# Output projection and first gate/up matrices of a hybrid encoder layer: side work as one list of timed events, four operands split in place, spatial matmuls interleaved

## The chip, the cores and the metric

The kernel is one program on one core of a Trainium2 chip. The time is the device time of one execution in microseconds (us). The engines of the core run their own instruction streams in order and wait for each other by semaphores: PE (TensorE, matmuls and transposes), DVE (VectorE), ACT (ScalarE), POOL (GpSimd) and SP (SyncE). Here SP issues nearly all DMA transfers, one after the other, and an issue that must wait holds back the issues behind it.

## The reference, cut to what matters

Two sequences of 1024 tokens (16 tiles of 128 tokens, 1024 wide) go through one encoder layer in fp32:

```python
h = rms_norm(x, norm1)
proj = h @ w_in                                   # q, k, v, gu, gv
a = rms_norm(windowed_gqa(q, k, v, ...), attn_out_gain)
g = rms_norm(chunked_spatial_gating(gu, gv, v_gain, w_s, b_s), gmlp_out_gain)
x = x + concatenate([a, g], -1) @ w_o             # output projection
h2 = rms_norm(x, norm2)
x = x + (silu(h2 @ w_gate) * (h2 @ w_up)) @ w_down
```

In `chunked_spatial_gating` each of 8 heads has a full 128x128 matrix that mixes the positions of a chunk: `s = einsum("hpq,bcqhd->bcphd", w_s, vh) + b_s`, and the result is `gelu(u) * s`.

## The kernel before

Every fp32 product is made of three fp16 (or fp32r) matmuls of split operands: a high part `hi`, which ACT casts, and a low part `lo = src - hi`, which DVE subtracts (`split16`, lines 112 to 114: one ACT and one DVE instruction each).

The stages that the change touches come after the attention:

**Gating loop**, `for t in range(NT)`. Tile `t` gets the products gv and gu (`gm_pieces`, 24 matmuls each). After every fourth tile, at t = 5, 9 and 13, `gm_group` applies the spatial matrices to a group of four tiles: 8 heads, 3 matmuls each into one of the 4 banks of the PSUM pool `psx`; DVE empties a bank with 2 instructions (line 684) before the fifth head can use it again. In between, `wo_step` and `wo_step2` load two rows of blocks of w_o (tiles `wr`, line 730), scale them on ACT (line 731) and split them.

**Output projection**, `for n in range(8): o_pair(n, ...)`. A pair is two tiles, q and q+4 of one sequence. The 2x2 block product is made of seven block products instead of eight, so a pair is 7 products of 12 matmuls, `o_product(ops, 0..6, ...)`. Its seven operands come from `o_turn`: load the two `mix` tiles (attention and gating halves, from DRAM), transpose them on PE (16 transposes `pm`), add and subtract blocks, and split. The finished rows `xr` are stored (`x1_d`), normalised (`o_norm`: square on ACT, power on POOL, scale on ACT into `xs`), and then `o_h2` transposes them (8 transposes `ph` for each tile), copies them to `hf` with the gain (8 small ACT instructions, line 957), forms the sums and differences of blocks and stores seven operands `B11, T2, B21, T3, T1, T4, B22` in DRAM (`t_d`).

**Gate/up matrices**, `matrix(n)`. The FFN's gate and up products have the same form: 7 products of 12 matmuls for each (weight pair, gate or up, sequence). Their operands `tops[s, i]` are read back from `t_d` (`top_load`: two loads of 512 KB for each operand into tiles `tr`) and split (`top_conv`: a cast on ACT and a subtraction on DVE of 1024 columns each). Operands 0 to 3 of a sequence lie in two tiles of the pool `big` (4 slots of 16 KB a partition), operands 4 to 6 in the pool tag L. The first two matrices (weight pair 0) run for sequence 0 alone, the next two (weight pair 1) for sequence 0 and then two for sequence 1. `prep_op` makes the seven weight operands of a matrix.

The order is the program order of the Python calls, refined by the framework's own scheduler: it keeps the emitted order as a priority and fills gaps. What stands between the products is set by hand: `POS = ['', 't', '', '0', '1', '']` says what follows each product of a pair: `o_turn` of the next pair after product 1, `o_h2` of the previous pair's two tiles after products 3 and 4. `pair_hooks` adds loads and conversions of sequence 0's operands for pairs 4 to 7; the rest of them, the preparation of the first weight operands and the last pair's `o_h2` come after pair 7. `top_step` does one load or conversion of sequence 1's operands after each product of the first four matrices.

The tags of the pool `k4p` limit what is in flight: XL has 3 slots (`mix` and `tr` share them), XN 3 (`xr`, and weights `raw` of up matrices), S 9, M 8, L 12.

Of the kernel before, what the change touches and what calls it, by code (L numbers as in the profile page):

```python
# [35 lines left out]
POS = ['', 't', '', '0', '1', '']  # L36
# [15 lines left out]

TW = {
# [11 lines left out]
def kernel(  # L65
# [461 lines left out]
    def gm_pieces(t, z):  # L527
        nm_ = ("gv", "gu")[z]
        if z == 0:
            pxg[t] = k4("S", f"xg{t}", (P, 2, GW))  # L530
        elif t % GROUP:
            pxg[t] = grp[t // GROUP][0][t % GROUP // 2][:, t % 2, :]
        ps = mm(f"p{nm_}{t}", [P, GW])
        for k in range(KD):
            mm3(ps, hT[t](k), wgl[nm_][0][:, k, :], wgl[nm_][1][:, k, :], k == 0, k == KD - 1)
            yield
        if z:
            dst = pxg[t] if t % GROUP else pxg[t][:, 1]
# [244 lines left out]
    def o_turn(n):  # L783
        xts, pms = [], []
        for t in pairs[n]:
            mx_ = k4("XL", f"mix{t}")
            load(mx_[:, 0:AW], mix_a[t])
            load(mx_[:, AW:D], mix_g[t])
            for z in range(2):
                pt = xx(f"pm{t}_{z}", [P, 4, P])  # L790
                for j in range(4):
                    k = z * 4 + j
                    nc.tensor.transpose(pt[:, j, :], mx_[:, k * P : (k + 1) * P], ident)
                pms.append(pt)
        for t in pairs[n]:
            xt = k4("XN", f"xr{t}")
            load(xt, xn[t])
            xts.append(xt)
        sc = h16(f"sc{n}", (P, 8, 4, P), F32)
        a11, a12, p21, a22 = pms  # L800
        a21, s1, s2, s3, s4 = (sc[:, i] for i in range(5))
        tl = [k4("S", f"mo{n}_{i}", (P, 2, 2, 4, P), F16) for i in range(4)]
        ops = [(tl[i // 2][:, i % 2, 0], tl[i // 2][:, i % 2, 1]) for i in range(7)]
        split16(*ops[0], a11)
        split16(*ops[2], a12)
        nc.scalar.copy(a21, p21)
        nc.vector.tensor_add(s1, a22, a21)
        split16(*ops[5], a22)
        nc.vector.tensor_sub(s3, a11, a21)
        nc.vector.tensor_sub(s2, s1, a11)  # L810
        split16(*ops[1], s2)
        nc.vector.tensor_sub(s4, a12, s2)
        split16(*ops[3], s3)
        split16(*ops[4], s1)
        split16(*ops[6], s4)
        st_b[n] = (xts, sc, ops)

    for t in range(NT):
        if t + 1 < NT and t + 1 >= NFILL:
            split_x(t + 1)  # L820
        if t >= NFILL:
            run(gm_pieces(t, 0))
        if t % GROUP:
            if t == 1:
                gm_chain(0)
            if t % GROUP != 1 or t == 1:
                gm_chain(t)
        if t > GROUP and t % GROUP == 1:
            gm_group(t // GROUP - 1)
            gm_chain(t - 1)  # L830
            gm_chain(t)
        if t == NT - 1:
            o_turn(0)
# [40 lines left out]
    def o_norm(t, xt):  # L874
        store(x1_d[t], xt)
        xs = k4("L", f"xs{t}")
        ms = small("a_ms", 1)
        nc.scalar.activation(xs, xt, AF.Square, scale=1.0 / 32.0, accum_out=ms)
        r2 = rsqrt_mean("a", ms, 1, EPS)
        nc.scalar.mul(xs, xt, r2)  # L880
        st_b["x", t] = xs

    def o_pair(n, hooks=()):
        (x_t, x_u), sc, ops = st_b.pop(n)
# [7 lines left out]
        def half(j):  # L892
            if n >= 1:
                o_h2(pairs[n - 1][j])

        def turn():
            if n + 1 < len(pairs):
                o_turn(n + 1)

        def extra(i):  # L900
            for fn in hooks[i] if hooks else ():
                fn()
            for c in POS[i]:
                if c == "0":
                    half(0)
                elif c == "1":
                    half(1)
                else:
                    turn()

        pa = mm(f"wa{n}", [P, 512])
        o_product(ops, 0, pa, True, True)
        nc.scalar.copy(u2, pa)
        extra(0)
        pb = mm(f"wb{n}", [P, 512])
        o_product(ops, 1, pb, True, True)
        nc.vector.tensor_add(u2, pb, u2)
        extra(1)
        o_product(ops, 2, pa, False, True)
        done(x_t, 0, pa)  # L920
        extra(2)
        pc = mm(f"wc{n}", [P, 512])
        o_product(ops, 3, pc, True, True)
        nc.scalar.copy(p7, pc)
        extra(3)
        pd = mm(f"wd_{n}", [P, 512])
        o_product(ops, 4, pd, True, True)
        nc.scalar.copy(p5, pd)
        nc.vector.tensor_add(p7, p7, u2)
        extra(4)  # L930
        o_product(ops, 5, pc, False, True)
# [4 lines left out]
        o_norm(pairs[n][1], x_u)  # L936
        extra(5)
        o_product(ops, 6, pd, False, True)
        nc.vector.tensor_add(u2, pd, u2)
        done(x_t, 1, u2)  # L940
        o_norm(pairs[n][0], x_t)

    hfs = {}

    def o_h2(t):
        s, i = divmod(t, TS)
        half, q = divmod(i, 4)
        xs = st_b.pop(("x", t))
        hf = k4("L", f"hf{t}", (P, KD, P))
        for z in range(2):  # L950
# [4 lines left out]
            for j in range(4):  # L955
                k = z * 4 + j
                nc.scalar.mul(hf[:, k, :], pt[:, j, :], n2s[:, k : k + 1])
        cs = slice(q * P, (q + 1) * P)
        if half == 0:
            hfs[t] = hf  # L960
            store(t_d[s][B11][:, :, cs], hf[:, 0:4, :])
            store(t_d[s][B21][:, :, cs], hf[:, 4:8, :])
# [3 lines left out]
        store(t_d[s][B22][:, :, cs], b22)  # L966
# [6 lines left out]
        for op, src in ((T1, ta[:, 0]), (T2, ta[:, 1]), (T3, tb[:, 0]), (T4, tb[:, 1])):  # L973
            store(t_d[s][op][:, :, cs], src)

    B11, T2, B21, T3, T1, T4, B22 = range(7)
    tops = {}
    top16 = {}
# [3 lines left out]
    def top_load(s, i, z, tag="XL"):  # L982
        traw[s, i, z] = k4(tag, f"tr{s}_{i}_{z}", (P, 2, 512))
        load(traw[s, i, z], t_d[s][i][:, 2 * z : 2 * z + 2, :])

    def top_conv(s, i, z):
        if z == 0:
            if i < 4:
                if i % 2 == 0:
                    top16[s] = h16(f"top{s}_{i}", (P, 2, 2, 4, 512), F16)  # L990
                tops[s, i] = (top16[s][:, i % 2, 0], top16[s][:, i % 2, 1])
            else:
                tops[s, i] = tuple(k4("L", f"top{s}_{i}{c}", (P, 4, 512), F16) for c in "hl")
        hi, lo = tops[s, i]
        raw = traw.pop((s, i, z))
# [78 lines left out]
    def product(key, s, i, ps, first, last):  # L1074
        op = wops[key, i]
        th, tl = tops[s, i]
        for k in range(4):
# [19 lines left out]

    tq = [(i, z) for i in range(7) for z in range(2)]
    tn = [0]

    def top_step():
        k = tn[0]
        tn[0] += 1
        if k % 2 == 0:
            if k >= 4:
                top_conv(1, *tq[k // 2 - 2])
            top_load(1, *tq[k // 2])
        elif k == 2 * len(tq) - 1:
            top_conv(1, *tq[-2])
            top_conv(1, *tq[-1])  # L1110
# [14 lines left out]
    def matrix(n):  # L1125
# [15 lines left out]
        def prep(i):  # L1141
            first, final = s == ss[0], s == ss[-1]
            if v == 0:
# [4 lines left out]
                top_step()  # L1148
                return
            if v == 1 and first:  # L1150
                if m == 0:
                    soon((1, 1), i)
                top_step()
# [39 lines left out]

        out_ = gate if m == 0 else up
        pa = bank(f"pa{nm}", [P, 512])
        product(key, s, 0, pa, True, True)
# [3 lines left out]
        product(key, s, 1, pb, True, True)  # L1200
        prep(1)
        nc.vector.tensor_add(u2, pb, u2)
        product(key, s, 2, pa, False, True)
# [3 lines left out]
        product(key, s, 3, pc, True, True)  # L1207
# [3 lines left out]
        product(key, s, 4, pd, True, True)  # L1211
# [3 lines left out]
        product(key, s, 5, pc, False, True)  # L1215
# [4 lines left out]
        product(key, s, 6, pd, False, True)  # L1220
# [20 lines left out]
    def pair_hooks(n):  # L1241
        if n < 4:
            return ()
        h = [[] for _ in range(6)]
        i = n - 4
        h[0].append(lambda: top_load(0, i, 0) if n > 4 else None)
        h[2].append(lambda: top_conv(0, i, 0) if n > 4 else None)
        h[3].append(lambda: top_load(0, i, 1) if n > 4 else None)
        h[5].append(lambda: top_conv(0, i, 1) if n > 4 else None)
        if n == len(pairs) - 1:  # L1250
            h[0].insert(0, lambda: load_raw((0, 0), "S"))
            h[4].append(lambda: top_load(0, 4, 0))
            h[5].append(lambda: top_load(0, 4, 1))
        return h

    for n in range(len(pairs)):
        o_pair(n, pair_hooks(n))
        if n == 4:
            top_load(0, 0, 0)
            top_load(0, 0, 1)  # L1260
            top_conv(0, 0, 0)
            top_conv(0, 0, 1)
    load_raw((0, 1))
    for i in range(7):
        prep_op((0, 0), i)
        if i == 3:
            top_load(0, 5, 0)
            top_conv(0, 4, 0)
            top_conv(0, 4, 1)
            top_load(0, 5, 1)  # L1270
            top_load(0, 6, 0)
    o_h2(pairs[-1][0])
    o_h2(pairs[-1][1])
    top_conv(0, 5, 0)
    top_conv(0, 5, 1)
    top_load(0, 6, 1)
    top_conv(0, 6, 0)
    top_conv(0, 6, 1)
# [237 lines left out]
```

## Time and profile before

| | |
|---|---|
| times without a profile | 1853.62 us median of 3 (1853.16 to 1853.8) |
| the profiled execution's own time | 1855.08 us |
| its span, first to last instruction | 1853.3 us |
| instructions | 26039 |
| PE busy | 1815.3 us (98%) |
| DVE / ACT busy | 1158.5 us (63%) / 1009.5 us (54%) |
| DMA | 282.05 MB, mean 152 GB/s |

The page gives, for one profiled execution, each engine's busy time, the span in slices, the chain of waits that ended last, and the costliest groups of instructions. Other views cut the same trace: busy time by stage (windows), waits by who waited for whom, instructions by line and shape, DMA issues, and the timeline. All times inside the trace count from the span's start.

### The profile page before, as it was taken

The numbers are of one execution on the slowest core, as the hardware profiler recorded it, in microseconds if no ns is written. First come the engines' busy times: TensorE is split into PE (matmuls) and PEld (weight loads), VectorE is DVE, ScalarE is ACT, GpSimd is POOL, SyncE is SP. The second block draws the span as 40 slices with busy tenths as digits, with TensorE's granted clock in tenths as the row PEclk, the third lists the DMA queues.
The fourth block names the chain that finished last, engine by engine and source line by source line (L and its number), as shares of the span: only waits on it lengthen the run. The fifth ranks groups of instructions, "written<-read, shape, count | busy, mean of one in ns | idle before, by whom it ended". The sixth has DMA issues, their size and how long they took to land.

```text
span 1853.3 us, 26039 instructions
## 1 busy us (share of the span) xinstructions
PE 1815.3 (98%) x9696; PEld 992.3 (54%) x9696; DVE 1158.5 (63%) x2183; ACT 1009.5 (54%) x1918; POOL 106.1 (6%) x139
## 2 busy tenths in 40 slices
PE   8999999999998999999999999999999999999999
PEld 7678767878554444444444444444444444444444
DVE  4988883665777896555545645645556956555761
ACT  6899997754666775444535534534444553333340
POOL 2122110111100000000000000000000000000000
PEclk9999999999999999999999999999999999999999
DMA  7799998432667874322313313313262764333641
GB/s 243 166 190 183 194 200 268 159 103 80 209 217 252 283 244 158 125 86 109 119 69 131 108 41 120 114 63 114 86 240 101 250 199 137 103 105 101 235 139 46
DMA packets 216027, 282.05 MB, mean 152 GB/s; under 512 B 103091, under 2 KB 137907, under 8 KB 215900
## 3 DMA queue, kind: packets, MB, share of 16 engines
q1 hardware_dynamic: 215724, 280.11, 49.4%
q8 instruction: 76, 1.25, 0.3%
q10 hardware_dynamic: 144, 0.26, 0.1%
q14 instruction: 51, 0.42, 0.1%
q0 software_dynamic: 32, 0.02, 0.0%
HBM read 177.04 MB, written 80.23 MB: 139 GB/s over the span
## 4 chain that ended last, share of the span: by engine, by line
PE 61%; DVE 2%; DMA 1%; ACT 1%; issue 0%; SPq 0%; POOL 0%; DVEq 0%
PE pd L1353 7%; PE pd L1355 7%; PE pd L1354 7%; PE pd L1079 4%; PE pd L1080 4%; PE pd L1081 4%; PE pa L1079 4%; PE pc L1079 4%; PE pa L1080 4%; PE pc L1080 4%; PE pc L1081 4%; PE pa L1081 4%; PE pb L1079 2%; PE pb L1080 2%; PE pb L1081 2%; DMA tr<-t_d 1%
## 5 line engine op out<-in xcount | busy, mean ns | idle before, releaser
L1355 PE MATMUL pd<-wop,a 128*128 128x512 f16 x616 | 233.5, 379 | 0.0
L1354 PE MATMUL pd<-wop,a 128*128 128x512 f16 x616 | 233.5, 379 | 0.0
L1353 PE MATMUL pd<-wop,a 128*128 128x512 f16 x616 | 233.5, 379 | 0.0
L1080 PEld LDWEIGHTS <-op 128*128 128x128 f16 x1232 | 120.6, 98 | 149.0 <-issue 7.4
L1081 PEld LDWEIGHTS <-op 128*128 128x128 f16 x1232 | 120.5, 98 | 146.5 <-issue 1.4
L1079 PEld LDWEIGHTS <-op 128*128 128x128 f16 x1232 | 122.3, 99 | 143.1 <-issue 0.3
L1079 PE MATMUL pa<-top,op 128*128 128x512 f16 x352 | 133.4, 379 | 0.5 <-ACT ua L1197 0.5
L1081 PE MATMUL pa<-top,op 128*128 128x512 f16 x352 | 133.4, 379 | 0.0
L1080 PE MATMUL pa<-top,op 128*128 128x512 f16 x352 | 133.4, 379 | 0.0
L121 ACT ACTIVATE wop<-wd,wdr_r 128x512 f16<-128x512 f32 x66 | 47.2, 720 | 150.9 <-PE pd L1355 147.4
L121 ACT ACTIVATE a<-as,asr_r 128x512 f16<-128x512 f32 x154 | 102.1, 710 | 33.6 <-DMA as<-act_d 15.4
L122 DVE SCALAR_TENSOR_TENSOR a<-as,asr_r,a 128x512 f16<-128x512 f32 x154 | 108.7, 746 | 6.3 <-ACT a L121 6.2
L1208 ACT COPY ub<-pc 128x512 f32<-128x512 f32 x44 | 25.7, 585 | 158.9 <-PE pc L1081 158.9
L122 DVE SCALAR_TENSOR_TENSOR wop<-wd,wdr_r,wop 128x512 f16<-128x512 f32 x66 | 49.2, 749 | 98.0 <-ACT wop L121 98.0
L1353 PEld LDWEIGHTS <-a 128*128 128x128 f16 x616 | 60.4, 98 | 72.5
L1355 PEld LDWEIGHTS <-a 128*128 128x128 f16 x616 | 60.3, 98 | 72.7
L1354 PEld LDWEIGHTS <-a 128*128 128x128 f16 x616 | 60.3, 98 | 72.6
L1022 ACT ACTIVATE junk_e<-g 128x1024 f32<-128x1024 f32 x44 | 46.3, 1053 | 70.4 <-DVE g L1192 70.4
L1214 DVE TENSOR_TENSOR ub<-ub,ua 128x512 f32<-128x512 f32 x44 | 30.4, 691 | 81.6 <-ACT ub L1208 79.2
L439 ACT ACTIVATE sc<-sc,mx 128x384 f32<-128x384 f32 (+1 forms) x128 | 74.3, 582 | 10.8 <-DVE mx L423 10.6
L1189 ACT ACTIVATE g<-g,rs 128x512 f32<-128x512 f32 x57 | 41.1, 721 | 62.5 <-DVE g L1224 35.5
L1079 PE MATMUL pd<-top_6h,op 128*128 128x512 f16 x176 | 66.7, 379 | 3.9 <-ACT ub L1212 3.7
(367 smaller groups left out, 4561.9 us busy)
## 6 DMA issues: line engine op xcount, KB each, us to landing
as<-act_d SPq DMA_DIRECT2D x77, 512.0 KB, 3.6
act_d<-g SPq DMA_DIRECT2D x66, 256.0 KB, 2.0
xs<-in_xT_dram SPq DMA_DIRECT2D x28, 512.0 KB, 4.4
tr<-t_d SPq DMA_DIRECT2D x28, 512.0 KB, 5.3
raw<-in_wg_dram SPq DMA_DIRECT2D x24, 512.0 KB, 4.0
raw<-in_wu_dram SPq DMA_DIRECT2D x24, 512.0 KB, 4.2
act_d<-sa SPq DMA_DIRECT2D x44, 256.0 KB, 2.5
act_d<-sb SPq DMA_DIRECT2D x44, 256.0 KB, 3.0
```

The source lines that it names most:

```text
L121: nc.scalar.mul(hi, src, gain)
L122: nc.vector.scalar_tensor_tensor(lo, src, gain, hi, ALU.mult, ALU.subtract)
L439: nc.scalar.activation(sc[:, v, :W], sc[:, v, :W], AF.Exp, bias=self.mn[:, h : h + 1], scale=-1.0, accum_out=self.sums[:, h : h + 1],)
L1022: nc.scalar.activation(junk_e[0], src, AF.Square, accum_out=acc)
L1079: nc.tensor.matmul(ps, op[:, 0, k, :], th[:, k, :], start=first and k == 0, stop=False, **more)
L1080: nc.tensor.matmul(ps, op[:, 0, k, :], tl[:, k, :], start=False, stop=False, **more)
L1081: nc.tensor.matmul(ps, op[:, 1, k, :], th[:, k, :], start=False, stop=last and k == 3, **more)
L1189: nc.scalar.activation(dst, src, AF.Silu, scale=iv)
L1214: nc.vector.tensor_add(p7, p7, u2)
L1353: nc.tensor.matmul(ps, a[:, 0, s, cs], wop[:, 0], start=first and n == 0, stop=False, **kw)
L1354: nc.tensor.matmul(ps, a[:, 0, s, cs], wop[:, 1], start=False, stop=False, **kw)
L1355: nc.tensor.matmul(ps, a[:, 1, s, cs], wop[:, 0], start=False, stop=end, **kw)
```

## The change

1. `o_turn` is cut in five: `mix_load`, `xr_load`, and `turn_a`, `turn_b`, `turn_c` (the same instructions, in three lots). `o_h2` is cut into `o_h2` (transposes and scaling) and `o_put` (sums, differences, and where they go). `o_norm` is called separately.
2. `POS`, `pair_hooks` and `top_step` go. Every such step is put with a time in one list, `do(time, fn, ...)`, in units of products: pair n begins at 7n, the first matrix at 56. Before each product of the pairs and of the first six matrices, `tick` runs all steps whose time has come.
3. For sequence 0, operands 0 to 3 are not stored in `t_d` and read back: `o_put` splits each 128-token piece straight into the operand's place (16 splits of 512 columns take the place of 16 stores of 256 KB, 8 loads of 512 KB and 8 conversions of 1024 columns).
4. In the gating loop, at t = 5, 9 and 13, the pieces of `gm_group` alternate with those of the gu product of tile t, instead of standing before it.
5. For tiles with `t % GROUP`, the target of gelu(gu) is looked up when it is written, instead of before the product.

By the new times the next pair's `mix` tiles are loaded 14 and 12 products before the pair begins (before: one pair's length), `turn_a` runs 6 products before it, `turn_b` 4 before, and `turn_c` (operands 4 and 6) after the pair's product 1. The `o_h2` of a pair's first tile runs before product 4 of the next pair, that of its second tile before product 1 of the pair after that; so the last pair's two tiles, and one tile of pair 6, are transposed between the products of the first two matrices. The first weight operands are prepared within pair 7.

The diff, cut to its core:

```diff
-POS = ['', 't', '', '0', '1', '']
+DT = dict(
+    mx0=-13.949, mx1=-11.679, xr0=-11.199, xr1=-7.545, ta=-5.743, tb=-3.638, tc=1.886, nu=8.268, nt=8.797, h0=10.459,
+    p0=13, h1=14.83, p1=15.401, raw0=45.957, raw1=54.748, prep=52.704, preps=0.249, tl=57.369, tls=0.412, tk=58.051,
+    tks=0.597, ul=64.811, uls=0.974, uk=67.481, uks=0.956,
+)
...
-    def o_turn(n):
-        xts, pms = [], []
+    mixes, xrs, pms = {}, {}, {}
+
+    def mix_load(t):
+        mixes[t] = k4("XL", f"mix{t}")
+        load(mixes[t][:, 0:AW], mix_a[t])
+        load(mixes[t][:, AW:D], mix_g[t])
+
+    def xr_load(t):
+        xrs[t] = k4("XN", f"xr{t}")
+        load(xrs[t], xn[t])
+
+    def turn_a(n):
...
         split16(*ops[0], a11)
         split16(*ops[2], a12)
         nc.scalar.copy(a21, p21)
         nc.vector.tensor_add(s1, a22, a21)
         split16(*ops[5], a22)
+    def turn_b(n):
...
         nc.vector.tensor_sub(s3, a11, a21)
         nc.vector.tensor_sub(s2, s1, a11)
         split16(*ops[1], s2)
         nc.vector.tensor_sub(s4, a12, s2)
         split16(*ops[3], s3)
+    def turn_c(n):
...
+        split16(*ops[4], sc[:, 1])
+        split16(*ops[6], sc[:, 4])
...
+        up = gm_pieces(t, 1)
         if t > GROUP and t % GROUP == 1:
-            gm_group(t // GROUP - 1)
+            group = gm_group_pieces(t // GROUP - 1)
+            while run(group, 1):
+                run(up, 1)
             gm_chain(t - 1)
             gm_chain(t)
...
-        run(gm_pieces(t, 1))
+        run(up)
...
+    def o_put(t):
...
+        def put(op, src):
+            if s == 0 and op < 4:
+                if op % 2 == 0 and (s, op) not in tops:
+                    top_pair(s, op)
+                hi, lo = tops[s, op]
+                split16(hi[:, :, cs], lo[:, :, cs], src)
+            else:
+                store(t_d[s][op][:, :, cs], src)
...
+        def mul(i, ps, first, last):
+            if n < 6:
+                tick(56 + 7 * n + i)
+            product(key, s, i, ps, first, last)
...
+    def do(time, fn, *args):
+        side.append((time, len(side), fn, args))
+
+    def tick(time):
+        while side and side[0][0] <= time:
+            _, _, fn, args = side.pop(0)
+            fn(*args)
+
+    for n, pair in enumerate(pairs):
+        T = 7 * n
+        for j, t in enumerate(pair):
+            if n:
+                do(T + DT[f"mx{j}"], mix_load, t)
+                do(T + DT[f"xr{j}"], xr_load, t)
+            do(T + DT["nt" if j == 0 else "nu"], o_norm, t)
+            do(T + DT[f"h{j}"], o_h2, t)
+            do(T + DT[f"p{j}"], o_put, t)
+        if n:
+            do(T + DT["ta"], turn_a, n)
+            do(T + DT["tb"], turn_b, n)
+            do(T + DT["tc"], turn_c, n)
+    do(DT["raw0"], load_raw, (0, 0), "S")
+    do(DT["raw1"], load_raw, (0, 1))
+    for i in range(7):
+        do(DT["prep"] + i * DT["preps"], prep_op, (0, 0), i)
+    for k in range(6):
+        do(DT["tl"] + k * DT["tls"], top_load, 0, 4 + k // 2, k % 2)
+        do(DT["tk"] + k * DT["tks"], top_conv, 0, 4 + k // 2, k % 2)
+    for k in range(14):
+        do(DT["ul"] + k * DT["uls"], top_load, 1, k // 2, k % 2)
+        do(DT["uk"] + k * DT["uks"], top_conv, 1, k // 2, k % 2)
```

More of the change, by code (lines that the diff above doesn't have):

```diff
@@ L832 @@
         if t == NT - 1:
-            o_turn(0)
-        run(gm_pieces(t, 1))
+            for q in pairs[0]:
+                mix_load(q)
+            turn_a(0)
+            for q in pairs[0]:
+                xr_load(q)
+            turn_b(0)
+            turn_c(0)
+        run(up)
         if 1 <= t < 5:
@@ L881, in o_norm, with o_pair, product @@
         st_b["x", t] = xs
-    def o_pair(n, hooks=()):
-        (x_t, x_u), sc, ops = st_b.pop(n)
+    def o_pair(n):
+        def product(i, ps, first, last):
+            tick(7 * n + i)
+            assert i in st_b[n][2]
+            o_product(st_b[n][1], i, ps, first, last)
+        sc = st_b[n][0]
+        x_t, x_u = (xrs.pop(t) for t in pairs[n])
         flat = [sc[:, i].rearrange("p a b -> p (a b)") for i in range(8)]
@@ L965, in o_h2 @@
         b11, b21, b12, b22 = h0[:, 0:4, :], h0[:, 4:8, :], hf[:, 0:4, :], hf[:, 4:8, :]
-        store(t_d[s][B22][:, :, cs], b22)
+        put(B22, b22)
         ta = k4("L", f"ta{t}", (P, 2, 4, P))
@@ L973, in o_h2 @@
         for op, src in ((T1, ta[:, 0]), (T2, ta[:, 1]), (T3, tb[:, 0]), (T4, tb[:, 1])):
-            store(t_d[s][op][:, :, cs], src)
+            put(op, src)
     B11, T2, B21, T3, T1, T4, B22 = range(7)
-    tops = {}
-    top16 = {}
+    tops, convs = {}, []
     traw = {}
@@ L983, in top_load, with top_pair @@
         traw[s, i, z] = k4(tag, f"tr{s}_{i}_{z}", (P, 2, 512))
+        assert s == 0 or len(puts) == NT
         load(traw[s, i, z], t_d[s][i][:, 2 * z : 2 * z + 2, :])
+    def top_pair(s, i):
+        pair = h16(f"top{s}_{i}", (P, 2, 2, 4, 512), F16)
+        for j in range(2):
+            tops[s, i + j] = (pair[:, j, 0], pair[:, j, 1])
     def top_conv(s, i, z):
@@ L1076, in product @@
         th, tl = tops[s, i]
+        assert s == 0 and i < 4 or (s, i, 1) in convs
         for k in range(4):
```

163 lines of the change are left out of this document (51 added, 112 removed).

## The prediction

> **What bounds the kernel now.** I read the page first, then busy time by stage (the columns are the stretch, its length, then busy us and instruction count of each engine, PE's clock, and DMA), with stages cut at the start of a product.
>
> ```profile
> PE 1815.3 (98%) x9696; PEld 992.3 (54%) x9696; DVE 1158.5 (63%) x2183; ACT 1009.5 (54%) x1918; POOL 106.1 (6%) x139
> ```
> ```profile
> 369.00:382.00 13.00, 8.52 (x38) 7.47 (x37) 10.02 (x27) 7.74 (x14) 0.00 (x0) 0.74 0.26 91
> 382.00:480.30 98.30, 97.40 (x473) 74.94 (x472) 59.80 (x143) 47.69 (x101) 15.26 (x22) 1.00 0.33 113
> 480.30:566.93 86.63, 86.63 (x466) 47.21 (x465) 63.67 (x107) 58.54 (x133) 5.70 (x8) 1.00 0.65 211
> 566.93:636.53 69.60, 64.17 (x334) 33.35 (x332) 54.82 (x85) 51.06 (x108) 6.00 (x6) 1.00 0.86 281
> 636.53:721.86 85.33, 77.27 (x353) 35.75 (x352) 67.63 (x93) 55.01 (x86) 1.10 (x2) 0.98 0.74 236
> 721.86:1853.30 1131.44, 1127.72 (x5255) 514.57 (x5253) 635.54 (x1026) 481.07 (x787) 16.36 (x23) 1.00 0.36 122
> ```
> ```profile
> 640.00:648.00 8.00, 5.71 (x27) 3.84 (x26) 3.03 (x5) 7.81 (x19) 1.10 (x2) 0.79 0.87 297
> ```
>
> PE is the bound; the change leaves its work as it is, so it can only win PE's idle and slow time. The rows are: spatial matrices of t = 9; the next gating tiles and pair 0; pairs 1 to 4; pairs 5 to 7; the first four matrices; the rest. The last row prices a matmul: 1131.44/5255 = 0.215 us, a product of 12 2.58 us. The pairs 1 to 4 lose nothing: 86.63/4 = 21.66 us for 7 products (18.1) and 32 transposes (3.5, 0.11 each). From that:
>
> - t = 9: idle 13.00 - 8.52 = 4.5 us, and a clock of 0.74 over 13 us costs up to 3.4 more; part of that falls on the idle time, so I take 2.9. Loss 7.4.
> - Pairs 5 to 7: three pairs less pair 7's missing turn (16 transposes) are 65.0 - 1.8 = 63.2. They take 69.6. Loss 6.4, of which 5.4 is idle (69.60 - 64.17); the rest goes where PE changes between matmuls and transposes.
> - First matrices: 28 products 72.3, two tiles' transposes 1.8, together 74.1. They take 85.33. Loss 11.2: idle 8.1, the clock of 0.79 over 8 us (1.7), mixing 1.4.
>
> Together 25.0 us. The next view, PE's waits in these stretches (engine, line, waited for: us, times, longest), names the causes.
>
> ```profile
> PE sg L679 <- DVE u L684: 4.5, 1, 4.5
> PE pm L793 <- DMA mix<-mix_a: 4.3, 2, 2.2
> PE wa L870 <- ACT sc L913: 1.1, 2, 0.7
> PE pd L1079 <- ACT ub L1212: 3.7, 2, 1.9
> PE ph L954 <- ACT xs L880: 2.3, 1, 2.3
> PE pd L1080 <- DVE top_6l L998: 0.9, 1, 0.9
> ```
>
> Set against the order of instructions that the changed kernel builds into, each cause stands as follows.
>
> **A. Spatial matmuls interleaved (t = 9).** The timeline shows why DVE was late:
>
> ```profile
> 366.30 0.68 DVE L114 TENSOR_TENSOR wo5l<-wr,wo5h 128x512 f16<-128x512 f32 x1
> 371.30 1.15 ACT L731 ACTIVATE wr<-wr,wgain 128x1024 f32<-128x1024 f32 x1 [0.30 <-DMA wr<-in_w_o_dram]
> 374.94 0.34 DVE L684 SCALAR_TENSOR_TENSOR u<-sg,cst,u 128x128 f32<-128x128 f32 x1
> ```
>
> A load of w_o can start only when DVE has freed its slot (366.98), lands at 371.3, ACT scales it, and DVE's in-order queue has four w_o instructions that hang on it ahead of the first emptying of an `sg` bank. PE fills its 4 banks and stops at the fifth head. In the changed order three stand ahead (a subtraction, wo4l, wo2l), and the instruction that frees the slot has moved up by 0 to 0.9 us, so DVE gets there at about 373.4 to 374.3 and has freed the first bank 0.6 us later. And PE now has four steps of gu among the first four heads:
>
> ```profile
> 366.67 0.39 PE L223 MATMUL pgv<-wgv_hi,xl 128*128 128x512 f32 x1
> 366.90 0.39 PE L221 MATMUL pgv<-wgv_hi,xh 128*128 128x512 f32 x1
> ...
> 369.62 0.28 PE L679 MATMUL sg<-vh,ws_hi 128*128 128x256 f32 x1
> ...
> 369.97 0.28 PE L679 MATMUL sg<-vh,ws_hi 128*128 128x256 f32 x1
> ```
>
> A step is 3 matmuls, 0.23 us apart, and a head 0.35, together 1.04: PE wants the fifth head at 369.62 + 4 x 1.04 = 373.8, and its bank is free at 374.0 to 374.9. The wait becomes 0.2 to 1.1 us; I take 0.5, too short to lower the clock. Gain 6.9. At t = 5 and 13 there was little to win, and the same alternation holds. Edit 5 (the target looked up later) changes no instruction.
>
> The clock: after 4.5 us of idleness it was low at 0.74, but also after the 2.3 us wait for `xs` (0.79 in 640 to 648). The Trainium skill, "TensorE: Matmul & The Clock Gate", section "HAM oscillation — how this bites in real kernels", gives the rule as no idle gaps over about 3.4 us; the second of these rows disagrees with it. By that rule the 1.7 us at 640 would have another cause and stay, and the time would come out 1.7 us higher.
>
> **B. Turn, mix and put (pairs).** Counts per pair: the turn, `o_norm` and `o_h2` issue the same instructions as before. The mix loads now stand ahead of SP's waits for `hf`, `ta`, `x1_d` and the `tr` loads, with `turn_a` about 20 us after them; a mix load takes about 5 us (row below). So both waits for `mix` (4.3) and the ACT waits (1.1) that come with late turns should go. New: 4 splits a pair in pairs 1 to 5.
>
> ```profile
> L114 DVE TENSOR_TENSOR mo<-sc,mo 128x512 f16<-128x512 f32 x16 | 9.9, 683 | 0.0
> L113 ACT CAST mo<-sc 128x512 f16<-128x512 f32 x16 | 9.1, 620 | 1.0 <-DVE sc L812 1.0
> L998 DVE TENSOR_TENSOR top<-tr,top 128x1024 f16<-128x1024 f32 x2 | 2.4, 1220 | 0.3 <-ACT top L997 0.3
> L997 ACT CAST top<-tr 128x1024 f16<-128x1024 f32 x2 | 2.1, 1045 | 2.6 <-DMA tr<-t_d 2.6
> L878 ACT ACTIVATE xs<-xr 128x1024 f32<-128x1024 f32 x9 | 9.5, 1052 | 15.0 <-issue 9.8 <-DVE xr L890 5.2
> L880 ACT ACTIVATE xs<-xr,a_r 128x1024 f32<-128x1024 f32 x8 | 9.1, 1146 | 5.4 <-POOL a_r L156 5.4
> ```
> ```profile
> xr<-in_xn_dram SPq DMA_DIRECT2D x13, 512.0 KB, 4.2
> tr<-t_d SPq DMA_DIRECT2D x11, 512.0 KB, 5.3
> t_d<-hf SPq DMA_DIRECT2D x21, 256.0 KB, 2.6
> mix<-mix_a SPq DMA_DIRECT2D x9, 256.0 KB, 4.9
> ```
>
> All 16 splits cost DVE 16 x 0.683 = 10.9 and ACT 16 x 0.620 = 9.9; 8 conversions less save 9.8 and 8.4. So DVE gets 1.1 and ACT 1.5 more, and 16 stores and 8 loads (8.4 MB) go. It is hidden where PE bounds: by the row for pairs 1 to 4, DVE is busy 63.67/4 = 15.9 and ACT 14.6 of 21.66 us; with four splits 18.6 and 17.1. In pairs 5 to 7 DMA was the crowded resource (0.86 of 16 engines); there some 4 MB of loads go.
>
> Sums do not show order, so I laid one middle pair end to end, from the end of its product 0, with the spacing (not the length) of successive rows:
>
> ```profile
> 635.96 0.60 DVE tb L971
> 645.55 2.51 ACT hf L957 x10
> ```
>
> DVE starts a 512-column instruction every 0.60 us, ACT a small `hf` every 0.25. Of a longer ACT row the next overlaps some 0.1 (two rows of the timeline under C start 0.95 apart, the first 1.04 long): a cast 0.52, a scale 1.05, a square with the read of its sum 1.14. ACT: copy and 8 `hf` to 2.7, two squares to 5.0, two casts and a copy to 6.5, scale 7.55, three casts (two of them new) 9.1, scale 10.2, three casts 11.7, copy of product 3 at 12.2 (PE wants it at 13.9), 8 `hf` and two casts 15.2, copy of product 4 at 15.7 (PE wants it at 16.45). The margin is thin, 0.75 us, but positive. `xr`: its slot comes free at 7.55, it lands 4.2 us later, DVE wants it at 17.1. So I expect almost no wait: residue 0.3 to 3, I take 1.0. Gain 6.4 - 1.0 = 5.4.
>
> **C. First matrices.** The last pair's `o_h2` stood behind product 1 of the first matrix, before its `xs` was scaled; PE waited 2.3 us and ran slow for 1.7 more. Now `xs` has two to three products' time: 4.0 us go. Of the rest, the two waits for `ub` (3.7) are ACT copies queued behind something late:
>
> ```profile
> 676.92 1.04 ACT L997 CAST top<-tr 128x1024 f16<-128x1024 f32 x1 [1.13 <-DMA tr<-t_d]
> 679.11 0.56 ACT L1212 COPY ub<-pd 128x512 f32<-128x512 f32 x1
> 717.70 1.04 ACT L997 CAST top_6h<-tr 128x1024 f16<-128x1024 f32 x1 [4.74 <-DMA tr<-t_d]
> 718.65 0.58 ACT L1212 COPY ub<-pd 128x512 f32<-128x512 f32 x1
> ```
>
> The last `tr` loads are issued one to two products (2.6 to 5.2 us) earlier relative to the matrices, so the second (1.9) should go. But this stretch stays tight: one tile more is transposed here (0.9 us of PE work, moved out of the pairs, so no net cost), with its four block sums on DVE (2.4). DVE then has 67.6 + 2.4 = 70.0 of 74.9 us: 93%. And the loads of operands 5 and 6 still wait for XL slots, and ACT still stands in front of `raw` loads from slots that `o_norm` frees late. Laid end to end I find PE waiting about 0.5 to 1.8 us at the first matrix's product 5 and 0.2 to 1 us at the third. Residue 3 (only these, and mixing) to 8 (all but the `xs` wait and its clock); I take 5. Gain 11.2 - 5 = 6.2.
>
> **Sum.** 6.9 + 5.4 + 6.2 = 18.5. The profiled execution took 1855.08, so 1836.6 by its own time; it stands 1.46 above the median of the runs, so 1835.1; I say 1835. Best ends (0, 0.3, 3 left over) give 21.7 and 1832. Something under 0.2% (3.7 us) I count as no change, about what a measurement of this kernel can tell.
>
> **Rivals.**
> - *The waits only move to the first matrices.* For: DVE at 93% there, and XL and XN keep their 3 slots. Then C gives only its `xs` part less new waits, say 1, and B 3: 1855.1 - 6.9 - 1 - 3 = 1844.2, on the median's scale 1843. Chance 0.10.
> - *The interleaving doesn't take hold.* The old build already alternated heads 5 to 8 with gu, and DVE still has w_o instructions ahead. If the w_o load lands 3 us later, A's 6.9 stay: 1842. Against: its slot is freed by the same DVE instruction, in the new order no later. Chance 0.08.
> - *Slower: the pairs stall on `xr` or on ACT.* Place: `done` for the pair's second tile, DVE in order, and behind it the sums that free PSUM for the next product; likewise ACT's copy of product 4, with 0.75 us of margin. `o_norm` now runs in the next pair, so XN's slots come free later, and SP may stand in a store's wait before `xr`. If load plus queue took over 17.1 - 7.55 = 9.5 us, every us beyond is lost per pair, and a wait over some 2.3 us costs 1.7 of clock as well. To end over 0.2% slower, 18.5 + 3.7 = 22.2 us must go, 3.2 a pair: it decides from about 11.8 us on. At 12 us: 7 x (2.5 + 1.7) = 29.4 lost against 18.5 won, 1853.6 + 10.9 = 1864.5. Against: 4.2 us to land, DMA less busy. Chance 0.07.
> - *Gains cancel against a few of these*, within 0.2%: 0.02.
>
> **Numbers.** Forecast 0.73, the two weak gains 0.18: faster 0.91. Same 0.02, slower 0.07. Low end 1830 (a little below the best ends), high end 1846, which takes in both weak gains.
>
> **What would show it.** Right: no PE wait over 1.2 us for `u` at t = 9 and no low clock there; no wait for `mix`; pairs 5 to 7 near 21.7 us each; no `ph` wait before the second product of the first matrix, which ends some 5 us sooner; about 8.4 MB less DMA; PE waits from the first matrix to the fourth of 3 to 5 us, on `ub`, `top_5` or `top_6`. Wrong: pairs 1 to 4 over 22 us each with DVE waiting for `xr`, PE waiting for ACT copies in each pair, or the first four matrices still at 83 us or more.

## The result, and the profile after

The changed kernel takes 1838.39 us (median of 4, 1838.07 to 1839.41) against 1853.71 before (median of 4): ratio 0.9908, 95% interval 0.9894 to 0.9921, 15.3 us less. Run again in a later session it gave 1838.5 and the same ratio. The number forecast was 1835.0, with a range from 1830 to 1846. The profiled execution took 1838.31 us, with a span of 1836.5.

Busy time by engine, from the page of the changed kernel:

```profile
PE 1809.5 (99%) x9696; PEld 988.4 (54%) x9696; DVE 1161.0 (63%) x2191; ACT 1005.3 (55%) x1926; POOL 104.5 (6%) x139
DMA packets 206427, 273.66 MB, mean 149 GB/s; under 512 B 102707, under 2 KB 129331, under 8 KB 206300
```

The same number of matmuls, and 282.05 - 273.66 = 8.4 MB less DMA, as counted. Now busy time by stage, cut at the start of the same products as before (stretch, length, busy us and instructions of PE, weight loads, DVE, ACT and POOL, PE's clock, DMA):

```profile
370.13:381.16 11.03, 8.63 (x50) 7.26 (x48) 8.22 (x21) 5.70 (x9) 0.00 (x0) 1.00 0.16 62
381.16:477.22 96.06, 94.37 (x457) 72.10 (x456) 61.69 (x149) 48.95 (x104) 13.11 (x22) 1.00 0.36 121
477.22:562.84 85.62, 85.62 (x457) 46.32 (x456) 69.44 (x117) 60.95 (x138) 6.66 (x8) 1.00 0.51 175
562.84:625.97 63.13, 63.13 (x334) 33.65 (x333) 49.55 (x83) 44.72 (x103) 5.27 (x6) 1.00 0.70 230
625.97:704.94 78.97, 75.78 (x361) 35.52 (x360) 69.65 (x95) 56.67 (x94) 1.71 (x2) 1.00 0.78 257
704.94:1836.50 1131.56, 1127.81 (x5255) 514.57 (x5253) 634.72 (x1025) 480.97 (x787) 16.39 (x23) 1.00 0.36 122
```

The first two rows need the kernel before cut in the same way, from the first spatial head of t = 9 to the gv product of t = 10, and on to pair 1:

```profile
369.62:385.37 15.75, 11.27 (x49) 9.71 (x48) 11.82 (x32) 8.49 (x16) 2.35 (x3) 0.78 0.22 75
385.37:480.30 94.93, 94.03 (x458) 72.19 (x457) 57.39 (x137) 46.46 (x97) 12.91 (x19) 1.00 0.33 114
```

So t = 9 gave 4.7 us, of which the next stretch took back 1.1; pairs 1 to 4 gave 1.0 (one tile's 8 transposes, about 0.9, moved out of them); pairs 5 to 7 gave 6.5, the first four matrices 6.4, the rest -0.1. Less the 0.5 us by which the first head came later, that is the 16.8 us between the spans. PE's waits from t = 9 to the fourth matrix, in the changed kernel (engine, line, waited for: us, times, longest):

```profile
PE sg L682 <- DVE u L687: 3.3, 3, 2.4
PE pa L1114 <- ACT ua L1221: 1.9, 1, 1.9
PE pc L1114 <- ACT ub L1232: 1.3, 2, 0.8
PE pgv L227 <- DVE xl L195: 0.8, 1, 0.8
```

Gone are the waits for `mix`, `xs`, `sc` and `top_6`; PE is never idle in pairs 1 to 7. What is left stands at t = 9 and in the matrices.

### The profile page after: what moved, and what is told of

Same layout as the page of the kernel before. It is cut to its first block, busy times and chain, and to the rows that moved or that the text cites. A ratio compares the mean times of both kernels' runs of the same rounds, so it can differ in the third digit from the quotient of the medians.

```text
span 1836.5 us, 26016 instructions
## 1 busy us (share of the span) xinstructions
PE 1809.5 (99%) x9696; PEld 988.4 (54%) x9696; DVE 1161.0 (63%) x2191; ACT 1005.3 (55%) x1926; POOL 104.5 (6%) x139
## 2 busy tenths in 40 slices
DMA packets 206427, 273.66 MB, mean 149 GB/s; under 512 B 102707, under 2 KB 129331, under 8 KB 206300
## 3 DMA queue, kind: packets, MB, share of 16 engines
q8 instruction: 76, 1.25, 0.3%
## 4 chain that ended last, share of the span: by engine, by line
PE 87%; DVE 6%; DMA 3%; ACT 2%; issue 1%; POOL 1%; SPq 0%; POOLq 0%; DVEq 0%; ACTq 0%
PE pd L1378 7%; PE pd L1376 7%; PE pd L1377 7%; PE pa L1114 4%; PE pa L1116 4%; PE pa L1115 4%; PE pd L1114 4%; PE pc L1114 4%; PE pd L1115 4%; PE pc L1115 4%; PE pc L1116 4%; PE pd L1116 4%; PE pq L225 2%; PE ps L422 2%; PE pb L1114 2%; PE pb L1115 2%
## 5 line engine op out<-in xcount | busy, mean ns | idle before, releaser
L125 ACT ACTIVATE a<-as,asr_r 128x512 f16<-128x512 f32 x154 | 101.9, 709 | 32.9 <-DMA as<-act_d 16.1
L1114 PE MATMUL pc<-top_5h,op 128*128 128x512 f16 x176 | 66.7, 379 | 1.3 <-ACT ub L1232 1.3
```

Of the source, the lines that this page charges most:

```text
L125: nc.scalar.mul(hi, src, gain)
L1114: nc.tensor.matmul(ps, op[:, 0, k, :], th[:, k, :], start=first and k == 0, stop=False, **more)
```

## Experiments

The kernel before had medians of 1854.6, 1855.8 and 1854.9 us in the three sessions of these runs (the first on one chip, the other two on another), so ratios to it are compared, and stages. A stage time comes from one profiled execution of each kernel. Stage times in us, read from the windows of each trace at the same products:

| kernel | t = 9 to 10 | pairs 1-4 | pairs 5-7 | first 4 matrices | median | ratio, interval |
|---|---|---|---|---|---|---|
| before | 15.75 | 86.63 | 69.60 | 85.33 | 1853.71 | |
| changed | 11.03 | 85.62 | 63.13 | 78.97 | 1838.39 | 0.9908, 0.9894-0.9921 |
| changed, again | 11.24 | 85.62 | 63.12 | 78.55 | 1838.5 | 0.9908, 0.9894-0.9921 |
| before + interleaving | 14.80 | 86.71 | 69.03 | 85.54 | 1854.88 | 1.0000, 0.9991-1.0009 |
| before + interleaving, pinned | 8.40 | 86.80 | 68.76 | 84.63 | 1848.8 | 0.9967, 0.9955-0.9980 |
| changed, old times | 14.85 | 86.81 | 69.90 | 80.96 | 1849.75 | 0.9974, 0.9963-0.9985 |
| changed, by DRAM | 11.66 | 85.62 | 67.35 | 79.93 | 1844.95 | 0.9941, 0.9928-0.9954 |
| changed, norms early | 11.26 | 90.70 | 69.75 | 84.17 | 1857.72 | 1.0010, 1.0000-1.0021 |
| changed, mix late | 11.10 | 85.62 | 63.12 | 77.81 | 1837.61 | 0.9904, 0.9889-0.9918 |
| before, 4 slots XL | 14.95 | 86.49 | 69.26 | 82.44 | 1856.68 | 1.0018, 1.0006-1.0029 |
| changed, w_o later | 8.40 | 85.62 | 63.12 | 78.40 | 1840.04 | 0.9913, 0.9898-0.9928 |
| changed, pinned | 8.40 | 85.62 | 63.12 | 78.02 | 1832.75 | 0.9878, 0.9864-0.9892 |
| pinned, conversions later | 8.40 | 85.62 | 63.12 | 79.38 | 1834.86 | 0.9888, 0.9873-0.9903 |
| pinned, conversions spread | 8.40 | 85.62 | 63.12 | 80.45 | 1835.64 | 0.9895, 0.9881-0.9908 |

### What is the interleaving worth?

**Before + interleaving**, edit 4 of the change alone:

```diff
+        up = gm_pieces(t, 1)
         if t > GROUP and t % GROUP == 1:
-            gm_group(t // GROUP - 1)
+            group = gm_group_pieces(t // GROUP - 1)
+            while run(group, 1):
+                run(up, 1)
```

> The kernel before with one edit: at t = 5, 9 and 13 each spatial matrix is followed by one step of the gu projection. The side work of the pairs and the operands' way through DRAM stay as they were. If the parts add, this alone wins what the traces show between t = 9 and pair 0, 91.2 us before against 87.6 after: 3.6 us, so about 1850.1. Rival: the gain at t = 9 is lost again in the pairs, which still wait for their mix loads: within 1 us of 1853.7. Rival: the stage was faster for another reason (the split looked up late): the wait for u at t = 9 stays at 4.5 us.

Nothing was won by the medians. Its trace waits 3.9 us for `u` where the changed kernel waits 2.4, with the same steps in the same order around it, and the clock is at half from 377.4 on (waits first, then the windows):

```profile
PE sg L678 <- DVE u L683: 4.8, 3, 3.9
```
```profile
377.40:384.23 6.83, 4.93 (x16) 4.39 (x17) 6.55 (x20) 2.67 (x5) 0.00 (x0) 0.50 0.00 0
```

The timelines show where the two part. First the changed kernel, then this one: the issue of two w_o loads, and the scaling that starts when the first has landed:

```profile
354.04 0.93 SPq L733 DMA_DIRECT2D wr<-in_w_o_dram  x2
357.50 1.15 ACT L734 ACTIVATE wr<-wr,wgain 128x1024 f32<-128x1024 f32 x1 [0.42 <-DMA wr<-in_w_o_dram]
373.14 1.15 ACT L734 ACTIVATE wr<-wr,wgain 128x1024 f32<-128x1024 f32 x1 [1.80 <-DMA wr<-in_w_o_dram]
```
```profile
354.93 0.93 SPq L729 DMA_DIRECT2D wr<-in_w_o_dram  x2
359.69 1.15 ACT L730 ACTIVATE wr<-wr,wgain 128x1024 f32<-128x1024 f32 x1 [1.04 <-DMA wr<-in_w_o_dram]
375.55 1.15 ACT L730 ACTIVATE wr<-wr,wgain 128x1024 f32<-128x1024 f32 x1 [2.00 <-DMA wr<-in_w_o_dram]
```

In both the loads go out 16.1 us ahead of the first head (370.13 and 371.02). The first lands 3.5 us later in one and 4.8 us in the other, and these 1.3 us are handed down the whole chain (load, scale, split, slot free, next load) to the scaling that VectorE's queue hangs on at t = 9. This explains the traced execution; that the other ten of this run lost their gain in the same way is not shown.

**Changed, again**, on another chip than that of the run before (so the expectation's condition was not met):

> The changed kernel itself, unaltered, on the chip on which the interleaving alone gave nothing (ratio 1.000) and the wait for u at t = 9 was 3.0 to 4.8 us with the very same instructions there. Theory: what the interleaving is worth hangs on when w_o's load lands, so the stage from t = 9 to t = 10 takes 11 to 15 us from execution to execution (half-speed clock after a long wait or not), while pairs 5 to 7 (63.1) and the first four matrices (79) come out as in the first profile; median 1838 to 1842. Rival: the stage is fixed by the order and takes 11.0 us again, 1838.4.

1838.5, stage 11.24, wait 2.6: nearer to the rival's 11.0 than to the spread I expected. With the traces of the changed order (this one, the first, and those of the old times, by DRAM, mix late and norms early), the wait for `u` was 2.4 to 3.0 us in five of them and 4.8 in one. With edit 4 alone counted in, the three longest (3.0, 3.9 and 4.8) come from one chip, and the three traces of the other chip wait 2.5 to 2.6. Whether the chip or the single execution decides how late the loads land was not tested.

**Changed, w_o later**, to take w_o's instructions out of the way at t = 9 (here, and in the next cut, two lines are put on one):

```diff
-WO_AT = (6, 8, 10, 12)       WO2_AT = (8, 10, 12, 14)
+WO_AT = (7, 9, 11, 13)       WO2_AT = (9, 11, 13, 15)
```

> The changed kernel with w_o's preparation one or two tiles later (WO_AT 7, 9, 11, 13 and WO2_AT 9, 11, 13, 15), so that no instruction on w_o stands among VectorE's instructions on the spatial matrices of t = 9; at t = 13 six of them now do. Theory: the 2.4 us wait left at t = 9, and the 0.8 us wait for xl two tiles later, are w_o's load landing at 373.1 with VectorE's queue behind it; both go, about 1835.5. Rival: the wait moves to t = 13, within 1 us of 1838.4 or slower.

Both happened. No time is lost at t = 9 any more, and the wait for `xl` behind it is gone, but instructions on w_o now stand among VectorE's on the heads of t = 13; PE waits 3.2 us there and the clock falls. The stretch from there to pair 0, second row, takes 37.9 us; it takes 32.4 in the kernel before and in the changed one:

```profile
371.49:379.89 8.40, 8.40 (x50) 7.35 (x48) 4.76 (x16) 0.74 (x2) 0.00 (x0) 1.00 0.00 0
417.97:455.88 37.91, 34.62 (x166) 28.49 (x164) 26.87 (x65) 22.50 (x48) 5.97 (x8) 0.95 0.43 148
```

**Changed, pinned.** The framework's scheduler had moved w_o's third step, emitted after t = 10, ahead of the heads of t = 9. The edit emits the step at the end of t = 9 and pins two of its subtractions behind what was emitted before them; that keeps it behind the heads, whenever its load lands:

```diff
-WO_AT = (6, 8, 10, 12)       WO2_AT = (8, 10, 12, 14)
+WO_AT = (6, 8, 9, 12)        WO2_AT = (8, 9, 12, 14)
-        split16(wo[0][0][:, k, :], wo[0][1][:, k, :], b11)
-        split16(wo[2][0][:, k, :], wo[2][1][:, k, :], b21)
+        for z, src in ((0, b11), (2, b21)):
+            hi, lo = wo[z][0][:, k, :], wo[z][1][:, k, :]
+            nc.scalar.copy(hi, src)
+            ins = nc.vector.tensor_sub(lo, src, hi)
+            if k == 2:
+                tc.keep_in_program_order(ins)
```

> The changed kernel, with VectorE's two differences of w_o's third step (wo0l, wo2l) pinned behind what was traced before them, so that all 16 instructions on u at t = 9 stand ahead of the step, and the step behind them but ahead of t = 13 (WO_AT 6, 8, 9, 12; WO2_AT 8, 9, 12, 14). Theory: the wait at t = 9 is that step's load; the stage from t = 9 to t = 10 takes 8.4 us, as at t = 5 and t = 13, and nothing moves to t = 13: 2.6 us less than the changed kernel at its best, 3 to 6 on this chip, and the runs scatter less. Rival: the delayed step makes VectorE or the next loads late for t = 13 or pair 0: within 1 us of the changed kernel.

```profile
368.18:376.58 8.40, 8.40 (x49) 7.35 (x48) 5.11 (x17) 3.73 (x6) 0.00 (x0) 1.00 0.20 76
```

1832.75 us (1832.05 to 1834.73), 5.75 less than the changed kernel on the same chip (1837.7 to 1839.57), and nothing moved to t = 13 (32.45). It is the fastest version here. Not all of the 5.75 is the pin's: in the traces the stage of t = 9 gives 2.6 and the next stretch 0.4 us, while the first head of t = 9 comes 1.95 us earlier (368.18 against 370.13), where the edit has changed nothing yet. In the two later runs of the pinned kernel with other times it came at 371.56 and 370.81.

**Before + interleaving, pinned**: both edits above on the kernel before.

> The kernel before with the interleaving and with w_o's third step pinned behind the instructions on u at t = 9, and nothing else of the change. Theory: the loss at t = 9 is as large as taken (7.4 us) and can be had in full once the load stands behind: the stage from t = 9 to t = 10 takes 8.4 us instead of 15.75, and the whole is 6.5 to 8 us under the kernel before. Rival: pairs 5 to 7, which wait for mix and ACT, take most of it back: 3 us or less.

The stage went from 15.75 to 8.40 us, 7.35 less: the loss of 7.4 at t = 9 was there, and could be had alone. The whole gained 6.1 us by the medians, a little under what was expected.

### Order or DRAM traffic?

**Changed, old times**: operands split in place, but the pairs' side work at the places of the kernel before.

```diff
-mx0=-13.949, mx1=-11.679, xr0=-11.199, xr1=-7.545, ta=-5.743, tb=-3.638, tc=1.886, nu=8.268, nt=8.797, h0=10.459, p0=13, h1=14.83, p1=15.401
+mx0=-5.3, mx1=-5.3, xr0=-5.1, xr1=-5.1, ta=-5.2, tb=-5, tc=-5, nu=6, nt=7, h0=11, p0=11, h1=12, p1=12
```

> The changed kernel with the times of the pairs' side work put back to where the kernel before had it (mix and xr loads at the turn, the whole turn ahead of product 2, norms right behind the sums, the h2 tiles ahead of products 4 and 5). Operands 0 to 3 are still split in place, without DRAM. Theory 1, the order made the gain: the waits for mix (2 x 2.2) come back in pairs 5 to 7, and part of the waits in the first matrices; 5 to 8 us slower than the changed kernel, 1844 to 1846. Theory 2, the smaller DMA traffic made it (16 stores and 8 loads less, so mix loads land earlier even where they start late): within 2 us of 1838.4.

Slower than both theories gave. In the traces 3.8 us of the difference stand at t = 9, which this edit doesn't touch (14.85 against 11.03). The waits for `mix` did not come back, so Theory 1 named the wrong wait; another stands in pairs 5 to 7, which take as long as before (waits, then the window):

```profile
PE wa L900 <- ACT sc L931: 4.0, 1, 4.0
```
```profile
567.30:637.20 69.90, 65.87 (x334) 34.25 (x333) 49.43 (x83) 44.68 (x100) 4.17 (x6) 0.95 0.63 208
```

**Changed, by DRAM**: new times, but all operands stored and read back.

```diff
-            if s == 0 and op < 4:
+            if False:
+    for k in range(8):
+        do(43.5 + k * 1.3, top_load, 0, k // 2, k % 2)
+        do(44.8 + k * 1.3, top_conv, 0, k // 2, k % 2)
```

> The changed kernel with its new times, but the first four operands of sequence 0 go through DRAM again: all stores are made, and 8 loads of 512 KB with their conversions are spread over products 43.5 to 54 of the list. Theory 1, the order made the gain: the stage of pairs 5 to 7 stays near 63 us, the whole within 2 us of 1838.4. Theory 2, the traffic made it: DMA in pairs 5 to 7 is back at 0.86 busy, PE waits there for mix or for ACT behind late loads, 4 to 7 us slower, 1843 to 1845.

DMA is back at 0.83, PE waits 2.3 us for `xs` and the clock falls; 4.2 us of the stage's 6.5 are lost. No wait for `mix` here either (window, then waits):

```profile
561.96:629.31 67.35, 65.02 (x333) 34.21 (x332) 53.88 (x84) 50.93 (x108) 4.89 (x6) 0.97 0.83 274
```
```profile
PE ph L966 <- ACT xs L911: 2.3, 1, 2.3
```

So in pairs 5 to 7 the new times without the splits in place won 2.3 us, the splits without the new times nothing, both together 6.5.

**Changed, norms early**: only `o_norm` goes back.

```diff
-nu=8.268, nt=8.797
+nu=6, nt=7
```

> The changed kernel with only the norms put back to where they were: the second tile's right behind its last sum (nu = 6), the first tile's right after product 6 (nt = 7). Theory, from the run with all the old times: the norms' squares and scalings then stand on ScalarE ahead of its copy of the next pair's product 0, PE waits about 4 us for it in the last pair and runs slow for up to 3.4 us after it; pairs 5 to 7 take 67 to 70 us instead of 63.1, the whole 1842.5 to 1845. Rival: that wait came from the other old times (the turn in one piece, the h2 tiles later): within 1 us of 1838.5.

The whole gain was lost, far more than I expected, and not in the last pair alone. The timelines show ScalarE's queue from product 0 of a pair on. In the changed kernel ScalarE copies product 0 at once, and takes both squares before the first scaling; with the norms early (second fence) the copy stands behind the whole norm of one tile and the square of the other, and the first scaling stands right behind its own square, where ScalarE idles 1.36 us for the power (`a_r`):

```profile
544.01 0.59 ACT L931 COPY sc<-wa 128x512 f32<-128x512 f32 x1 [5.68 <-PE wa L902]
544.49 2.18 ACT L969 ACTIVATE hf<-ph,n2s 128x128 f32<-128x128 f32 x8
546.50 1.12 ACT L909 ACTIVATE xs<-xr 128x1024 f32<-128x1024 f32 x1
...
547.54 1.12 ACT L909 ACTIVATE xs<-xr 128x1024 f32<-128x1024 f32 x1
...
550.00 1.24 ACT L911 ACTIVATE xs<-xr,a_r 128x1024 f32<-128x1024 f32 x1
```
```profile
546.11 1.06 ACT L909 ACTIVATE xs<-xr 128x1024 f32<-128x1024 f32 x1 [3.30 <-DVE xr L927]
547.07 0.19 ACT L909 ACTIVATION_READ_ACCUMULATOR xs<-xr 128x1 f32 x1
548.62 1.15 ACT L911 ACTIVATE xs<-xr,a_r 128x1024 f32<-128x1024 f32 x1 [1.36 <-POOL a_r L160]
549.67 1.04 ACT L909 ACTIVATE xs<-xr 128x1024 f32<-128x1024 f32 x1
550.62 0.18 ACT L909 ACTIVATION_READ_ACCUMULATOR xs<-xr 128x1 f32 x1
550.71 0.56 ACT L931 COPY sc<-wa 128x512 f32<-128x512 f32 x1
...
552.78 2.16 ACT L969 ACTIVATE hf<-ph,n2s 128x128 f32<-128x128 f32 x8
```

PE's waits in the pairs, and pairs 1 to 4 as a window:

```profile
PE pm L805 <- ACT hf L969: 6.0, 8, 1.7
PE wa L900 <- ACT sc L931: 2.6, 1, 2.6
```
```profile
478.61:569.31 90.70, 86.72 (x458) 46.21 (x457) 67.62 (x117) 62.73 (x138) 5.71 (x8) 1.00 0.48 165
```

ACT is at work for only 62.7 of 90.7 us, so it is the order in its queue, not its load, that holds PE: the transposes of the turn wait for the banks that `hf` frees late.

**Changed, mix late**: `mx0=-5.76, mx1=-5.75`.

> The changed kernel with one thing put back: the mix loads stand again right ahead of the turn's transposes (8 and 6 products' time later than in the changed kernel). Theory 1, the early mix loads took away the waits for mix: 2 waits of about 2.2 us come back in pairs 5 to 7, 4 to 5 us slower than the changed kernel. Theory 2, the emptier DMA queue took them away (with the old times and no trip through DRAM there was no wait for mix): within 1 us of the changed kernel.

This told nothing: the scheduler issued the loads at the same point in both. The last mix load of the last turn goes out 20.2 us ahead of the first transpose here and in the changed kernel.

**Before, 4 slots XL**: `slots = {..., "XL": 4, ..., "S": 8}`.

> The kernel before with a fourth slot XL for loads of 512 KB (and one slot S less, for space). Theory: the mix loads of the last two turns were late because the loads of operands 0 to 3 held the XL slots, not because of where the list of instructions had them; both waits for mix (2 x 2.2 us) go, pairs 5 to 7 take 64 to 66 us instead of 69.6, the whole 3 to 6 us less than before. Rival: they stood in SP's queue behind stores; the waits stay, within 1 us of before (or slower, if the missing slot S hurts).

A miss. The waits for `mix` fell from 4.3 to 1.3 us, but ScalarE's copies came late instead (`wa`, `wd`: 3.7 us), and pairs 5 to 7 took 69.3. So the slots were a part of the cause of those waits and not all of it, and nothing was won on the whole. The copies came late with one slot S less; whether that slot is why was not tested. The timeline of the kernel before shows SP issuing the last turn's mix loads behind four stores of the sums and a store of `x1_d`:

```profile
593.74 0.89 SPq L974 DMA_DIRECT2D t_d<-tb  x1
594.72 0.96 SPq L875 DMA_DIRECT2D x_d<-xr  x1
595.77 0.80 SPq L787 DMA_DIRECT2D mix<-mix_a  x1
```

### The rest of the first matrices

Two attempts on the waits of 1.9 us (`ua`) and 1.3 us (`ub`) that are left in the changed kernel, both made on the pinned kernel, in whose trace they are only 1.0 and 1.2: `uk=69.0` (conversions later), and `uls=1.25, uks=1.25` (loads and conversions spread).

> The pinned kernel, and the conversions of sequence 1's operands 1.5 products later (uk from 67.481 to 69.0), so that fewer of them stand on ScalarE ahead of its copy of product 0 of the third matrix, for which PE waited 1.9 us. Theory: that wait goes, 1 to 2 us less than the pinned kernel. Rival: another conversion or a sum of squares takes its place in ScalarE's queue: within 0.7 us of the pinned kernel.

> The pinned kernel with the loads and conversions of sequence 1's operands spread wider (one per 1.25 products instead of 0.97 and 0.96). Theory: the waits of 0.5 to 1 us for copies in the third and fourth matrix, which stand behind conversions waiting for their loads, shrink: 1 to 1.5 us less than the pinned kernel, about 1831.5. Rival: the last conversions now collide with the loads of the next matrices for the XL slots: slower by 1 us or more.

Both are misses. The first moved the waits (1.3 for `ua`, 1.7 for `ub`, 79.4 us for the stage), the second lengthened one to 2.0 us, with a clock loss behind it (80.5). Why `ub`'s copy is late there stays open.

## Why the prediction was right, and where it was not

- **The sum** was 18.5 us by the profiled executions; they differ by 1855.08 - 1838.31 = 16.8. Another 1.5 us of the miss is the offset: I took 1.46 us off because the profiled execution of before lay that far above the median. That of the changed kernel lies 0.1 below its own. It was chance in one execution, and no cost of being profiled: in the twelve later runs the profiled execution lay between 2.7 us under and 2.5 over the median. The number came as close as it did because errors cancelled: A gave 3.3 us less than forecast, and the stretches of B and C and pairs 1 to 4 together 2.2 more.
- **A, spatial matmuls: 6.9 forecast, 4.7 measured, 3.6 after what came back at `xl`.** This is the step that failed. I held that the instruction that frees the slot would come 0 to 0.9 us earlier, and the wait be 0.5 us. It was 2.4. The step had moved up in the order of instructions, but it hangs on a load that SP issued 16.1 us ahead of the first head, and 19.3 in the kernel before: it came 0.8 us later (1.83 us ahead of the first head instead of 2.63). Then the load that waits for the slot took 0.5 us longer, from its issue to ScalarE's scaling: 4.8 us in the changed kernel (to 373.14) where it had been 4.3 (to 371.30). Together that is 1.3 to 2.2 us more than forecast. (The two issues stand below this list.) The clock stayed at full speed, as forecast, but by luck: the wait straddled two windows (last section). The rival "the interleaving doesn't take hold" had the mechanism, and in the run of edit 4 alone nothing was won. That the 7.4 us could be had was right: pinned, all of it is.
- **B, pairs: 5.4 forecast, 6.5 measured.** Right, with no residue at all instead of 1.0. The cause was partly right: SP's queue. Either of the two edits, the new times or the splits in place, takes the waits for `mix` away, so which of them did it in the changed kernel can't be told. The 1.0 us put down to PE's switching between matmuls and transposes went too, though PE still switches there: it was no fixed cost of switching. The engines' sums were off: VectorE got 2.5 us more and ScalarE 4.2 less, where +1.1 and +1.5 were counted.
- **C, first matrices: 6.2 forecast, 6.4 measured**, with waits of 3.2 us on ACT's copies, within the 3 to 5 given. The `xs` wait went, and the clock of the whole stretch is 1.00. One more tile is transposed there (about 0.9 us, gone from pairs 1 to 4), so like for like it gave 7.3. No run isolates the cause: every changed kernel takes 78 to 81 us here, with the old times and by DRAM too, except with the norms early (84.2).
- **The rival that the waits only move** to the matrices did not come about: A, B and C all gave something.
- **The slower rival** named two places. VectorE never waits for `xr` in pairs 1 to 7. The other, ACT's queue, is real, though not at the copy of product 4 that was named: with the norms about two products earlier PE waits for `hf` and for the copy of product 0, and 17 to 19 us are lost (by the stages and by the medians).

The issues of the load that VectorE's queue hangs on at t = 9, before and changed; 371.30 and 373.14, where ScalarE starts on it, are in the timelines shown above:

```profile
367.02 0.33 SPq L730 DMA_DIRECT2D wr<-in_w_o_dram  x1
```
```profile
368.32 0.33 SPq L733 DMA_DIRECT2D wr<-in_w_o_dram  x1
```

## What to carry to other kernels

Where an in-order engine frees PSUM banks, look for what hangs on a transfer ahead of those instructions in its queue, and pin it behind them; its place in the instruction order says little if the transfer's issue moved. Two edits that each win little can be worth much together: here each took the waits for `mix` away, but alone it came with another wait (4.0 us for `sc` with the splits alone, 2.3 us for `xs` with the new times alone). Test them in both combinations. And the place of an instruction pair with a round trip in it (a square, a power on another engine, a scaling) can matter more than the engine's busy share: 5.1 us were lost in pairs 1 to 4 with ScalarE busy for 69% of them.

## What the runs showed of the hardware

The half-speed clock comes in stretches of 3.41 us on a fixed grid of each execution. In the 14 traces, from 260 us on, 83 windows of that grid at full clock held over 0.9 us of PE idleness: after all 25 with 1.98 us or more the next window ran at half, after none of the 58 with 1.92 or less. Before 260 us this border doesn't hold: three windows near 245 us with only 1.2 to 1.5 us of idleness (before, w_o later, 4 slots XL) were followed by half speed, and two near 45 us with 1.97 and 1.98 (changed, old times) were not. What counts there beside idleness stays open. So a wait's length alone does not tell. A wait of 2.3 us inside one window cost clock (before, first fence); one of 2.4 us that straddled two did not (the changed kernel at t = 9, second fence):

```profile
640.98:644.39 3.41, 1.12 (x9) 0.67 (x7) 0.15 (x1) 3.41 (x5) 0.71 (x2) 1.00 0.95 354
644.39:647.81 3.42, 3.42 (x15) 2.60 (x14) 2.36 (x2) 3.42 (x12) 0.00 (x0) 0.50 0.76 236
```
```profile
372.91:376.33 3.42, 1.58 (x9) 1.01 (x7) 2.00 (x4) 3.19 (x5) 0.00 (x0) 1.00 0.00 0
376.33:379.74 3.41, 2.85 (x17) 2.57 (x18) 3.41 (x12) 1.33 (x3) 0.00 (x0) 1.00 0.00 0
```

The rule of the Trainium skill, "TensorE: Matmul & The Clock Gate", section "HAM oscillation — how this bites in real kernels", that idle gaps over about 3.4 us bring the clock down, is too generous by these rows: two microseconds in the wrong place are enough.

A load of 512 KB, issued at the same point with the same work around it, took 3.5 us in one execution, 4.8 in another and 5.7 in a third (changed, before + interleaving, changed with old times). The two longer ones are from one chip; on the same chip it also took 3.5 (changed, by DRAM).
